# A hybrid decoder layer: transposing reads for the features of B and x, and SyncE's loads in program order

## The chip, the cores and the metric

The kernel runs on one core of a Trainium2 chip. The core has TensorE (PE; its weight loads are listed as PEld), VectorE (DVE), ScalarE (ACT), GpSimd (POOL) and SyncE (SP), which issues most DMAs. The metric is the device time of one launch in microseconds (us), lower is better.

## The reference

One decoder layer for 256 tokens of width 2048, in float32: a gated feed-forward network (FFN 1), a mixing block, a cross attention to 256 memory tokens and a second FFN, each added to the stream h, then a last RMSNorm. The mixing block has two halves that share one input projection `w_in`:

```python
proj = rmsnorm(h, mix_norm) @ w_in          # columns: u | v | z | x | B | C | dt
a = gelu(u) * (W_s @ rmsnorm(gelu(v)) + b)  # W_s causal in chunks of 128 tokens, 4 groups
x, B, C = split(silu(causal_conv4(x | B | C)))
dt = softplus(dt + dt_bias)
m = ssd_scan(x, dt, A, B, C) + d_skip * x   # 32 heads of 64, 8 groups, state 128, chunks of 128
m = rmsnorm(m * silu(z))
h = h + concat([a, m]) @ w_out
```

The scan works on two chunks of 128 tokens: inside a chunk a masked product of decays and scores with x * dt, between the chunks a state made of B and x * dt.

## The kernel before, in words

Every product in float32 is made of a high and a low half in float32r. A weight tile of 128 x 2048 elements is loaded (`load`, L136, on SyncE's queue, three buffers `raw`), cast to its high half by ScalarE (`high`, L166) and subtracted to its low half by VectorE (`low`, L179). Each projection is a loop over the inner dimension; one turn is a step, with its load, its split and its matmuls, and then `step()` (L82) runs what was put off with `later(fn, by)`: work that becomes due so many steps on. So the program order of all side work is written as due times. The scheduler of the language then orders each engine's instructions by their place in the program and by when it thinks they are ready; `behind(...)` holds an instruction behind named ones on its engine. Before the change, `behind` is used for the casts (`last_cast`) and for VectorE's splits (`last_split`, in `split_op`, L175), but not for DMAs.

The order of the mixing block:

- the B and C features, four column blocks of 512 with four steps each (`proj_feat`, L324): the output has features on partitions and tokens along the row. `gather` (L727) adds the banks, `conv_silu` (L739) makes the convolution and SiLU;
- `b_tokens` (L830): B's first chunk is wanted with tokens on partitions. Two steps after its column block, four TensorE transposes by an identity go into one PSUM bank and a copy brings them into `btok`, which `scan_states` reads much later;
- the x features, four column blocks of the same kind, into tiles `xf` of two feature tiles each. `x_tokens` (L847) turns them by four TensorE transposes each, two or three steps later, into one bank, and two copies bring them into `y[0]` and `y[1]`, the token tiles of the two chunks;
- v (16 steps, `proj_tok`, L212), then u (16 steps), then z (16 steps). The scan's four pieces are put off from the start of v: `scan_start` (L872) makes `xdt` = y * dt and y * d_skip for a chunk and reads the decay rows, `scan_decay` follows 1.5 steps later, `scan_apply` (L899) is due at 8, 12, 18.5 and 23;
- the output projection `w_out` (`add_sum`, L573), which reads the operands `at` (from a) and `mt` (from m).

There is a second way to turn a tile, used before for the FFNs' hidden tiles, for half of the mixing projection's operand and for a's operand: `turn_over` (L377) calls `write_planes` (L365), in which ScalarE copies the float32 tile into two planes of 16-bit halves (`halves`) and GpSimd writes them to DRAM (`planes`, four buffers); some steps later `read_turned` (L374) reads them with a transposing DMA on SyncE's queue into a tile `turned`, and again some steps later a `put` casts and splits that tile into an operand. The puts stand in line with the weights' casts and splits (`in_turn`, L388). The two due times are the pair `by`: (1, 4) for the hidden tiles, (2.5 + 1.5 n, 2.5) for chunk n of the mixing operand, (2.5 + 1.5 j, 2.5) for a's column j; the second of the two reads of a tile comes half a step after the first.

Of the kernel before, what the change touches and what calls it, by code (L numbers as in the profile page):

```python
# [8 lines left out]
F32 = mybir.dt.float32  # L9
F32R = mybir.dt.float32r  # L10
U16 = mybir.dt.uint16
# [6 lines left out]
P = 128  # L18
# [29 lines left out]
def hybrid_layer(ctx: ExitStack, tc: tile.TileContext, x, xt, mem, memt, w_gu1, w_dn1, w_in, w_s, w_out,  # L48
# [84 lines left out]
    PLAIN = {(0, 0): 0, (0, 1): 1, (1, 0): 2, (1, 1): 3}  # L133
    FOR_SUMS = {(0, 0): 0, (1, 0): 1, (1, 1): 2, (0, 1): 3}

    def load(w, r0, cs, at, fine=False):  # L136
        raw = wraw.tile([P, 2 * KP, NC], F32, name="raw")
        rows = w[r0:r0 + KP * P, :]
        if at is PLAIN and cs[1] == cs[0] + NC:
            nc.sync.dma_start(out=raw.rearrange("p (k j) n -> p k j n", j=2), in_=rows[:, cs[0]:cs[0] + 2 * NC].rearrange(  # L140
                "(k p) (j n) -> p k j n", p=P, j=2))
            return raw
        if fine:
            for (k, j), b in at.items():
                nc.sync.dma_start(out=raw[:, b, :], in_=rows[k * P:(k + 1) * P, cs[j]:cs[j] + NC])
            return raw
        for j, c in enumerate(cs):
            b, e = at[0, j], at[1, j]
            src = rows[:, c:c + NC]
            if e > b:  # L150
                nc.sync.dma_start(out=raw[:, b:e + 1:e - b, :], in_=src.rearrange("(k p) n -> p k n", p=P))
                continue
            for k, x in enumerate((b, e)):
                nc.sync.dma_start(out=raw[:, x, :], in_=src[k * P:(k + 1) * P, :])
        return raw

    def behind(instructions):

        order = ExitStack()
        for ins in instructions:  # L160
            order.enter_context(tc.issue_after(ins))
        return order

    last_cast = []

# [158 lines left out]
    def proj_feat(w, xts, n0):  # L324
        ps = {}
        n = D // P // (2 * KP)
        for i in range(n):
            raw = wraw.tile([P, 2 * KP, NC], F32, name="raw")
            nc.sync.dma_start(out=raw, in_=w[2 * i * KP * P:2 * (i + 1) * KP * P, n0:n0 + NC].rearrange(
                "(k p) n -> p k n", p=P))  # L330
            hi, lo = split(raw)
            order = [(k, c) for k in range(2 * KP) for c in range(4)]
            if i in (0, n - 1):
                order.sort(key=lambda kc: kc[1])
            for a in range(0, len(order), 4):
                for w_part in (hi, lo):
                    for k, c in order[a:a + 4]:
                        kt = 2 * i * KP + k
                        if c not in ps:
                            ps[c] = side("acc")  # L340
                        xt = xts[kt // KG][:, kt % KG, :]
                        w_kc = w_part[:, k, c * P:(c + 1) * P]
                        if w_part is hi:
                            matmul(ps[c], w_kc, xt, start=kt == 0)
                        else:
                            matmul(ps[c][:, S:], w_kc, xt[:, :S], stop=kt == D // P - 1)
            step()
        return [ps[c] for c in range(4)]
# [22 lines left out]
            nc.gpsimd.dma_start(out=planes[t * P:(t + 1) * P].rearrange("p b n -> p (b n)"), in_=halves)  # L371
        return planes

    def read_turned(to, planes, c0, n):  # L374
        nc.sync.dma_start(out=to, in_=planes[:, :, c0:c0 + n].rearrange("s b n -> (s b) n"), transpose=True)

    def turn_over(srcs, by, put):  # L377
        planes = write_planes(srcs)

        def fetch(q):  # L380
            to = half_k(F32, "turned")
            read_turned(to.bitcast(U16).rearrange("p (k s) -> p k s", k=KP), planes, q * P, KP * P)
            later(lambda: put(to.rearrange("p (k s) -> p k s", k=KP), q), by=by[1], bankless=True)

        for q in (0, 2):
            later(lambda q=q: fetch(q), by=by[0] + q / 4, bankless=True)

    def in_turn(src, last, op, c0=None):  # L388

# [66 lines left out]
    class Pieces(dict):  # L456
# [59 lines left out]
                                             op=ALU.subtract)  # L516
            return hi.ins, lo.ins

        def turn_later(self, srcs, by, c0=None, at=None):
            if at is None:  # L520
                at = self.due
                self.due += 2
            turn_over(srcs, by, lambda to, q: self.put(at + q // 2, to, q, c0))

        def later(self, srcs, c0=None, by=1):
            for q in (0, 2):
# [2 lines left out]
    class Normed:  # L529
# [8 lines left out]
        def chunk(self, n, by=1):  # L538
            srcs = [h[n][:, t, :] for t in range(NT)]
            if n < 2 and not isinstance(self.xts, Pieces):  # L540
                operand_turned(srcs, self.xts, f"xt_{self.name}{n}", self.c0 + n * KG, (2.5 + 1.5 * n, 2.5))
                self.stats(n)
            elif isinstance(self.xts, Pieces):

                for i in (2 * n, 2 * n + 1):
                    later(lambda i=i: self.xts.put(i, srcs, i % 2 * KP, self.c0 + n * KG),
                          self.bys.get(i, by))
                later(lambda: self.stats(n), self.stats_by)
            else:
                operand_later(srcs, self.xts, f"xt_{self.name}{n}", self.c0 + n * KG, by)  # L550
                self.stats(n)
# [59 lines left out]
    def ffn(nrm, w_gu, w_dn, done=None, each=None, fine=0, by_token=False):  # L611
        for c_from, c_to in ((0, 5), (5, 11)):
            kinds, turn = DN_KINDS[c_to - c_from]
            hts = Pieces(kinds, "hid", nrm.xts)
            for c in range(c_from, c_to):
                m = {}
                gs = []

                def mid(banks):
                    m["m1"], m["y"], m["z"], m["y2"] = parts_of(banks)  # L620

                def evac(t, j, ps):
                    g, u = (m["z"], m["y2"]) if t else (m["m1"], m["y"])
                    if j == 0:
                        total(g, ps, g, ALU.subtract if t else ALU.add)
                        nc.scalar.activation(g, g, AF.Silu, scale=nrm.rstd[:, t:t + 1])
                        return
                    total(u, ps, u)
                    nc.vector.scalar_tensor_tensor(out=g, in0=u, scalar=nrm.rstd[:, t:t + 1], in1=g,
                                                   op0=ALU.mult, op1=ALU.mult)  # L630
                    gs.append(g)

                if c == 0:
                    proj_sum(w_gu, 0, nrm.xts, FIRST_KINDS, (c * NC, DFF + c * NC), mid, evac, FIRST, fine)
                else:
                    proj_sum(w_gu, 0, nrm.xts, GU_KINDS, (c * NC, DFF + c * NC), mid, evac, GU_ORDER)
                hts.turn_later(gs, (1, 4))
            last = c_to == 11
            add_sum(w_dn, c_from * NC, hts, (kinds, kinds), turn, 0.5, done if last else None, each if last else None,
                    last and by_token)  # L640

# [186 lines left out]
    bt = slot([P, GROUPS, S], F32, "bt")  # L828
    ctr = slot([P, GROUPS, S], F32, "ct")
    def b_tokens(q):  # L830
        ps = side("tpose")
        for i in range(4):
            transpose(out=ps[:, i * P:(i + 1) * P], in_=bt[:, q * 4 + i, :P], identity=ident)
        nc.any.tensor_copy(out=btok[:, q * 4:q * 4 + 4, :], in_=ps.rearrange("p (g n) -> p g n", n=P))

    for c in range(4):
        xis = gather(proj_feat(w_in, nx.xts, B0 + c * NC))
# [3 lines left out]
        for i in range(4):  # L841
            conv_silu(xis[i], 16 + c * 4 + i, dst[:, (c % 2) * 4 + i, :])
        if c < 2:
            later(lambda c=c: b_tokens(c), by=2)
    y = [slot([P, HEADS, HD], F32, f"y{t}") for t in range(NT)]

    def x_tokens(c, i0, xf):  # L847
        tps = side("tpose").rearrange("p (t k s) -> p t k s", t=NT, k=2)
        for t in range(NT):
            for i in range(2):  # L850
                transpose(out=tps[:, t, i, :], in_=xf[:, i, t * P:(t + 1) * P], identity=ident)
        for t in range(NT):
            h0 = (c * 4 + i0) * 2
            nc.any.tensor_copy(out=y[t][:, h0:h0 + 4, :],
                               in_=tps[:, t].rearrange("p k (h d) -> p (k h) d", d=HD))

    for c in range(4):
        xis = gather(proj_feat(w_in, nx.xts, X0 + c * NC))
        for i0 in (0, 2):
            xf = half_k(F32, "xf").rearrange("p (k s) -> p k s", k=2)  # L860
            for i in range(2):
                conv_silu(xis[i0 + i], c * 4 + i0 + i, xf[:, i, :])
            later(lambda c=c, i0=i0, xf=xf: x_tokens(c, i0, xf), by=2 + i0 // 2)


    def per_head(ap, n):
# [5 lines left out]
    def scan_start(t, j):  # L872
        if j == 0:
            scan["xdt"] = scan[f"xdt{t}"] = xdt = slot([P, HEADS, HD], F32, "xdt")
            nc.vector.tensor_tensor(out=xdt, in0=y[t], in1=per_head(dt[:, t, :], HD), op=ALU.mult)
            nc.vector.tensor_tensor(out=y[t], in0=y[t], in1=per_head(rowb[:, 2, :], HD), op=ALU.mult)
        dec = slot([P, 16, P], F32, "dec")
        nc.gpsimd.dma_start(
# [60 lines left out]
                            base=0, channel_multiplier=-1)  # L939
    v = [slot([P, 4, NC], F32, f"v{t}") for t in range(NT)]  # L940
    ss_v = small.tile([P, NT, 4], F32, name="ss_v", bufs=1)
    for i, (by, to) in enumerate(((3, 8), (8, 12), (14, 18.5), (18.5, 23))):
        later(lambda i=i: scan_start(i // 2, i % 2), by=by)
        later(lambda i=i: scan_apply(i // 2, i % 2), by=to)
    for c in (0, 2):
# [31 lines left out]
    for c in (0, 2):  # L977
# [10 lines left out]

        proj_tok(w_in, 0, nx.xts, (U0 + c * NC, U0 + (c + 1) * NC), evac)
        for j in range(2):  # L990
            ats.turn_later(gss[j], (2.5 + 1.5 * j, 2.5))

    ss_m = small.tile([P, NT, 4], F32, name="ss_m", bufs=1)
    for c in (0, 2):
# [230 lines left out]
```

## Time and profile before

| | |
|---|---|
| time, median of 3 runs | 2428.43 us (2428.28 to 2432.98) |
| the profiled execution's own time | 2428.32 us |
| its span, first to last instruction | 2426.6 us |
| PE / DVE / ACT / POOL busy | 2413.6 / 2033.3 / 1361.4 / 65.4 us |
| granted TensorE clock | 0.999 |
| DMA traffic | 510 MB, mean 210 GB/s |
| transposing reads (`turned<-planes`) | 56 |

The page gives the busy time of each engine, the chain of work that ended last, and groups of instructions as "line engine operation out<-in". A timeline line has the start in us, the length in us, the engine, the line, the operation, out<-in, the tile's shape, a count, and in brackets the idle time of the engine before it with what ended it. For SPq the operation is the issue of a DMA, and the length is how long the queue was held by it and those merged with it. A line of the waits has who waited for whom, the sum in us, how many times and the longest. A line of the DMA issues has the count, the size of one and the median time from issue to landing. A matmul's printed length is longer than the distance to the next one's start, since they overlap. In the mixing block, the features lie from about 711 to 886 us, and v begins at 886.

### The profile page before, as it was taken

What the parts mean: (1) busy time and instruction counts of PE and PEld (TensorE: products, weight loads), DVE (VectorE), ACT (ScalarE), POOL (GpSimd) and SP (SyncE); (2) the same over time, 40 slices, a digit from 0 to 9 for tenths busy, and PEclk for the clock granted to TensorE, in tenths of its full rate; (3) what the DMA queues carried; (4) which work ended last, traced back from release to release, by engine and by line L of the source; (5) the groups of instructions that cost most, each with busy time, mean ns of one, the idle gap of its engine ahead of it and who ended that gap; (6) DMA issues with size and microseconds to landing.
All of it is one profiled execution on the core that took longest, in us unless ns stands there. A gap on an engine that the chain in (4) does not pass through costs nothing.

```text
span 2426.6 us, 29016 instructions
## 1 busy us (share of the span) xinstructions
PE 2413.6 (99%) x11141; PEld 2010.1 (83%) x11141; DVE 2033.3 (84%) x1943; ACT 1361.4 (56%) x1261; POOL 65.4 (3%) x124
## 2 busy tenths in 40 slices
PE   9999999999999999999999999999999999999998
PEld 7888888888888888788888888888888888888886
DVE  8999889999877777655698888778899988899997
ACT  7565446555656555445555655555556644556554
POOL 1000000000000000000000000000000000000000
PEclk9999999999999999999999999999999999999999
DMA  8777667677765555567557655555567776777774
GB/s 306 234 225 232 202 208 232 220 231 231 232 196 187 181 191 175 205 194 224 190 191 244 224 191 167 176 178 174 191 217 235 225 222 197 223 229 223 233 221 151
DMA packets 264844, 510.17 MB, mean 210 GB/s; under 512 B 75760, under 2 KB 77840, under 8 KB 263936
## 3 DMA queue, kind: packets, MB, share of 16 engines
q1 hardware_dynamic: 256224, 479.00, 62.6%
q0 software_dynamic: 7648, 28.26, 3.2%
q8 instruction: 87, 1.43, 0.2%
q10 hardware_dynamic: 832, 1.05, 0.1%
q14 instruction: 53, 0.43, 0.0%
HBM read 476.76 MB, written 16.81 MB: 203 GB/s over the span
## 4 chain that ended last, share of the span: by engine, by line
PE 95%; issue 3%; ACT 1%; DVE 1%; DMA 0%; SPq 0%; POOL 0%; POOLq 0%; DVEq 0%; ACTq 0%
PE acc L74 92%; PE tpose L77 1%; PE yp L74 1%; PE o L74 0%; PE logits L74 0%; PE mixed L74 0%; DVE lo L177 0%; DMA raw<-in_w_in 0%; ACT hi L169 0%; DMA raw<-in_w_gu 0%; PE dt L74 0%; PE scores L74 0%; PE yo L74 0%; PE st L74 0%; ACT hi L191 0%
## 5 line engine op out<-in xcount | busy, mean ns | idle before, releaser
L177 DVE TENSOR_TENSOR lo<-raw,hi 128x2048 fp32r<-128x2048 f32 (+2 forms) x449 | 945.2, 2107 | 242.5 <-PE acc L74 175.4
L169 ACT CAST hi<-raw 128x2048 fp32r<-128x2048 f32 (+1 forms) x437 | 785.0, 1798 | 488.6 <-PE acc L74 418.4
L74 PE MATMUL acc<-hi,xp_ffn 128*128 128x512 f32 x1824 | 574.3, 390 | 0.0
L74 PEld LDWEIGHTS acc<-hi,xp_ffn 128*128 128x128 f32 x1824 | 342.6, 188 | 71.1
L169 ACT CAST hi<-sum 128x2048 fp32r<-128x2048 f32 x117 | 224.1, 1915 | 294.8 <-DVE sum L177 153.4
L74 PE MATMUL acc<-lo,xp_ffn 128*128 128x512 f32 x912 | 355.0, 389 | 1.3 <-DVE h L661 1.3
L177 DVE TENSOR_TENSOR lo<-sum,hi 128x2048 fp32r<-128x2048 f32 x117 | 268.1, 2292 | 37.4 <-ACT hi L169 37.4
L74 PE MATMUL acc<-hi,hid 128*128 128x512 f32 x896 | 281.3, 389 | 0.0
L74 PE MATMUL acc<-hi,xt_mix 128*128 128x512 f32 x768 | 241.5, 393 | 0.0
L74 PEld LDWEIGHTS acc<-lo,xp_ffn 128*128 128x128 f32 x912 | 171.3, 188 | 37.5 <-DVE h L661 1.7
L600 DVE TENSOR_TENSOR part<-acc,part 128x512 f32<-128x512 f32 x272 | 180.5, 686 | 23.6 <-PE acc L74 8.5
L74 PEld LDWEIGHTS acc<-hi,hid 128*128 128x128 f32 x896 | 168.1, 188 | 34.9
L74 PE MATMUL acc<-lo,hid 128*128 128x512 f32 x448 | 174.3, 389 | 0.0
L74 PEld LDWEIGHTS acc<-hi,xt_mix 128*128 128x128 f32 x768 | 144.2, 188 | 30.8 <-issue 1.0
L177 DVE TENSOR_TENSOR sum<-sum,raw 128x512 f32<-128x512 f32 x234 | 161.6, 691 | 6.2
L74 PE MATMUL acc<-lo,xt_mix 128*128 128x512 f32 x384 | 149.7, 390 | 1.1 <-DVE lo L177 1.1
L74 PE MATMUL acc<-hi,xp_ffn1s 128*128 128x512 f32 x466 | 148.5, 389 | 0.0
L74 PE MATMUL acc<-hi,xp_ffn2s 128*128 128x512 f32 x466 | 148.5, 389 | 0.0
L177 DVE TENSOR_TENSOR sum<-raw 128x1024 f32<-128x1024 f32 x117 | 142.5, 1218 | 0.0
L74 PE MATMUL acc<-xt_mix,hi 128*128 128x512 f32 x512 | 140.5, 396 | 0.0
L74 PE MATMUL acc<-hi,hids 128*128 128x512 f32 x392 | 125.2, 389 | 0.0
L74 PE MATMUL acc<-hi,memt 128*128 128x512 f32 x384 | 123.4, 392 | 0.0
(297 smaller groups left out, 3164.6 us busy)
## 6 DMA issues: line engine op xcount, KB each, us to landing
raw<-in_w_gu SPq DMA_DIRECT2D x284, 512.0 KB, 4.6
raw<-in_w_in SPq DMA_DIRECT2D x80, 1024.0 KB, 5.1
raw<-in_w_dn SPq DMA_DIRECT2D x60, 1024.0 KB, 5.2
raw<-in_w_gu SPq DMA_DIRECT2D x136, 256.0 KB, 4.9
raw<-in_w_kv SPq DMA_DIRECT2D x24, 1024.0 KB, 5.2
raw<-in_w_out SPq DMA_DIRECT2D x21, 1024.0 KB, 5.2
planes<-halves POOLq DMA_DIRECT2D x56, 256.0 KB, 4.6
raw<-in_w_dn SPq DMA_DIRECT2D x28, 512.0 KB, 4.1
```

The lines of the kernel that those rows point to most:

```text
L74: return pe(nc.tensor.matmul(out, lhsT=lhsT, rhs=rhs, start=start, stop=stop))
L77: return pe(nc.tensor.transpose(out=out, in_=in_, identity=identity))
L169: last_cast[:] = [nc.scalar.copy(out=t[:, :n], in_=x[:, :n]).ins]
L177: last_split[:] = [nc.vector.tensor_tensor(**kw).ins]
L600: nc.vector.tensor_tensor(out=out, in0=a, in1=b, op=op)
```

## The change

It has four parts.

1. All weight loads and most transposing reads go through `from_dram`. From the first half of FFN 1 on (`line["kept"]`), each of them is held behind the one before it in the program, on SyncE's queue. The reads of the FFNs' hidden tiles and the new reads of B and x stay out of this line (`lined=False`).
2. The lined reads are one step apart (`q / 2`) and start later; their puts follow one step after: (6 + 2 n, 1) for the mixing operand, (6 + 2 j, 1) for a's.
3. `b_tokens` and `x_tokens` use no TensorE transposes and no PSUM any more: planes of 16-bit halves are written at once, and transposing reads bring them straight into `btok` (due one step later) and into `y[0]` (one step later) and `y[1]` (three steps later).
4. The scan's pieces are due later, and `xdt` stands in line with VectorE's splits.

```diff
+    line, last_load = {"kept": False}, []
+
+    def from_dram(lined=True, **kw):
+        with behind(last_load if lined and line["kept"] else ()):
+            ins = nc.sync.dma_start(**kw).ins
+        if lined:
+            last_load[:] = [ins]
...
-    def read_turned(to, planes, c0, n):
-        nc.sync.dma_start(out=to, in_=planes[:, :, c0:c0 + n].rearrange("s b n -> (s b) n"), transpose=True)
-
-    def turn_over(srcs, by, put):
+    def read_turned(to, planes, c0, n, lined=True):
+        from_dram(lined, out=to, in_=planes[:, :, c0:c0 + n].rearrange("s b n -> (s b) n"), transpose=True)
+
+    def turn_over(srcs, by, put, lined=True):
...
         for q in (0, 2):
-            later(lambda q=q: fetch(q), by=by[0] + q / 4, bankless=True)
+            later(lambda q=q: fetch(q), by=by[0] + (q / 2 if lined else q / 4), bankless=True)
...
-                operand_turned(srcs, self.xts, f"xt_{self.name}{n}", self.c0 + n * KG, (2.5 + 1.5 * n, 2.5))
+                operand_turned(srcs, self.xts, f"xt_{self.name}{n}", self.c0 + n * KG, (6 + 2 * n, 1))
...
-                hts.turn_later(gs, (1, 4))
+                hts.turn_later(gs, (1, 4), lined=False)
             last = c_to == 11
+            line["kept"] = True
...
     def b_tokens(q):
-        ps = side("tpose")
-        for i in range(4):
-            transpose(out=ps[:, i * P:(i + 1) * P], in_=bt[:, q * 4 + i, :P], identity=ident)
-        nc.any.tensor_copy(out=btok[:, q * 4:q * 4 + 4, :], in_=ps.rearrange("p (g n) -> p g n", n=P))
+        planes = dram.tile([P, 2, NC], U16, name="planes", tag="planes", bufs=4)
+        halves = tmp.tile([P, 2 * NC], U16, name="halves", tag="t2k")
+        halves_v = halves.rearrange("p (b g n) -> p b g n", b=2, g=4)
+        for g in range(4):
+            nc.scalar.copy(out=halves_v[:, :, g, :],
+                           in_=bt[:, q * 4 + g, :P].bitcast(U16).rearrange("p (n b) -> p b n", b=2))
+        nc.gpsimd.dma_start(out=planes.rearrange("p b n -> p (b n)"), in_=halves)
+        later(lambda: read_turned(btok[:, q * 4:q * 4 + 4, :].bitcast(U16), planes, 0, NC, False), by=1, bankless=True)
...
-            later(lambda c=c: b_tokens(c), by=2)
+            b_tokens(c)
...
     def x_tokens(c, i0, xf):
-        tps = side("tpose").rearrange("p (t k s) -> p t k s", t=NT, k=2)
-        for t in range(NT):
-            for i in range(2):
-                transpose(out=tps[:, t, i, :], in_=xf[:, i, t * P:(t + 1) * P], identity=ident)
-        for t in range(NT):
+        planes = write_planes([xf[:, i, :] for i in range(2)], S)
+
+        def fetch(t):
             h0 = (c * 4 + i0) * 2
-            nc.any.tensor_copy(out=y[t][:, h0:h0 + 4, :],
-                               in_=tps[:, t].rearrange("p k (h d) -> p (k h) d", d=HD))
+            read_turned(y[t][:, h0:h0 + 4, :].bitcast(U16).rearrange("p h d -> p (h d)"), planes, t * P, P, False)
+
+        for t in range(NT):
+            later(lambda t=t: fetch(t), by=1 + 2 * t, bankless=True)
...
-            later(lambda c=c, i0=i0, xf=xf: x_tokens(c, i0, xf), by=2 + i0 // 2)
+            x_tokens(c, i0, xf)
...
-            nc.vector.tensor_tensor(out=xdt, in0=y[t], in1=per_head(dt[:, t, :], HD), op=ALU.mult)
+            split_op(out=xdt, in0=y[t], in1=per_head(dt[:, t, :], HD), op=ALU.mult)
...
-    for i, (by, to) in enumerate(((3, 8), (8, 12), (14, 18.5), (18.5, 23))):
+    for i, (by, to) in enumerate(((4.5, 9), (9, 13), (15, 19.5), (19.5, 24))):
...
-            ats.turn_later(gss[j], (2.5 + 1.5 * j, 2.5))
+            ats.turn_later(gss[j], (6 + 2 * j, 1))
```

More of the change, by code (lines that the diff above doesn't have):

```diff
@@ L134, in hybrid_layer, with behind @@
     FOR_SUMS = {(0, 0): 0, (1, 0): 1, (1, 1): 2, (0, 1): 3}
+    def behind(instructions):
+        order = ExitStack()
+        for ins in instructions:
+            order.enter_context(tc.issue_after(ins))
+        return order
+    line, last_load = {"kept": False}, []
[4 more added lines that the diff above has]
+            last_load[:] = [ins]
     def load(w, r0, cs, at, fine=False):
@@ L139, in load @@
         if at is PLAIN and cs[1] == cs[0] + NC:
-            nc.sync.dma_start(out=raw.rearrange("p (k j) n -> p k j n", j=2), in_=rows[:, cs[0]:cs[0] + 2 * NC].rearrange(
+            from_dram(out=raw.rearrange("p (k j) n -> p k j n", j=2), in_=rows[:, cs[0]:cs[0] + 2 * NC].rearrange(
                 "(k p) (j n) -> p k j n", p=P, j=2))
@@ L144, in load @@
             for (k, j), b in at.items():
-                nc.sync.dma_start(out=raw[:, b, :], in_=rows[k * P:(k + 1) * P, cs[j]:cs[j] + NC])
+                from_dram(out=raw[:, b, :], in_=rows[k * P:(k + 1) * P, cs[j]:cs[j] + NC])
             return raw
@@ L150, in load @@
             if e > b:
-                nc.sync.dma_start(out=raw[:, b:e + 1:e - b, :], in_=src.rearrange("(k p) n -> p k n", p=P))
+                from_dram(out=raw[:, b:e + 1:e - b, :], in_=src.rearrange("(k p) n -> p k n", p=P))
                 continue
             for k, x in enumerate((b, e)):
-                nc.sync.dma_start(out=raw[:, x, :], in_=src[k * P:(k + 1) * P, :])
+                from_dram(out=raw[:, x, :], in_=src[k * P:(k + 1) * P, :])
         return raw
[L157 to L162, printed above, removed]
     last_cast = []
@@ L328, in proj_feat @@
             raw = wraw.tile([P, 2 * KP, NC], F32, name="raw")
-            nc.sync.dma_start(out=raw, in_=w[2 * i * KP * P:2 * (i + 1) * KP * P, n0:n0 + NC].rearrange(
+            from_dram(out=raw, in_=w[2 * i * KP * P:2 * (i + 1) * KP * P, n0:n0 + NC].rearrange(
                 "(k p) n -> p k n", p=P))
@@ L381, in fetch @@
             to = half_k(F32, "turned")
-            read_turned(to.bitcast(U16).rearrange("p (k s) -> p k s", k=KP), planes, q * P, KP * P)
+            read_turned(to.bitcast(U16).rearrange("p (k s) -> p k s", k=KP), planes, q * P, KP * P, lined)
             later(lambda: put(to.rearrange("p (k s) -> p k s", k=KP), q), by=by[1], bankless=True)
         for q in (0, 2):
-            later(lambda q=q: fetch(q), by=by[0] + q / 4, bankless=True)
+            later(lambda q=q: fetch(q), by=by[0] + (q / 2 if lined else q / 4), bankless=True)
     def in_turn(src, last, op, c0=None):
@@ L517, in sums, with turn_later @@
             return hi.ins, lo.ins
-        def turn_later(self, srcs, by, c0=None, at=None):
+        def turn_later(self, srcs, by, c0=None, at=None, lined=True):
             if at is None:
@@ L522, in turn_later @@
                 self.due += 2
-            turn_over(srcs, by, lambda to, q: self.put(at + q // 2, to, q, c0))
+            turn_over(srcs, by, lambda to, q: self.put(at + q // 2, to, q, c0), lined)
         def later(self, srcs, c0=None, by=1):
@@ L843, in hybrid_layer @@
         if c < 2:
-            later(lambda c=c: b_tokens(c), by=2)
+            b_tokens(c)
     y = [slot([P, HEADS, HD], F32, f"y{t}") for t in range(NT)]
     def x_tokens(c, i0, xf):
-        tps = side("tpose").rearrange("p (t k s) -> p t k s", t=NT, k=2)
+        planes = write_planes([xf[:, i, :] for i in range(2)], S)
+        def fetch(t):
+            h0 = (c * 4 + i0) * 2
+            read_turned(y[t][:, h0:h0 + 4, :].bitcast(U16).rearrange("p h d -> p (h d)"), planes, t * P, P, False)
         for t in range(NT):
-            for i in range(2):
-                transpose(out=tps[:, t, i, :], in_=xf[:, i, t * P:(t + 1) * P], identity=ident)
-        for t in range(NT):
-            h0 = (c * 4 + i0) * 2
-            nc.any.tensor_copy(out=y[t][:, h0:h0 + 4, :],
-                               in_=tps[:, t].rearrange("p k (h d) -> p (k h) d", d=HD))
+            later(lambda t=t: fetch(t), by=1 + 2 * t, bankless=True)
     for c in range(4):
```

## The prediction, made before the result was known

> **What bounds the kernel now.** I began with the page: its first part and the chain that ended last.
>
> ```profile
> span 2426.6 us, 29016 instructions
> ...
> PE 2413.6 (99%) x11141; PEld 2010.1 (83%) x11141; DVE 2033.3 (84%) x1943; ACT 1361.4 (56%) x1261; POOL 65.4 (3%) x124
> ...
> PE 95%; issue 3%; ACT 1%; DVE 1%; DMA 0%; SPq 0%; POOL 0%; POOLq 0%; DVEq 0%; ACTq 0%
> ```
>
> TensorE has work in 99% of the span and carries 95% of the chain. So an edit counts in two ways only: it takes matmul slots off TensorE, or it changes how long TensorE waits. Next, the view of the waits, for TensorE alone, shows how little waiting there is to win:
>
> ```profile
> PE idle L74 <- DVE idle L666: 1.3, 1, 1.3
> PE acc L74 <- DVE h L661: 1.3, 1, 1.3
> PE acc L74 <- DVE lo L177: 1.1, 1, 1.1
> ```
>
> Two of the three belong to L661 and L666, the opening of the kernel, which the change does not touch. The third, on a low half (L177), is the one that an edit could remove. Its place is in the timelines of TensorE, SyncE's queue and ScalarE around 1126 us, in the z projection:
>
> ```profile
> 1125.14 0.39 PE L74 MATMUL acc<-hi,xt_mix 128*128 128x512 f32 x1
> 1125.37 0.39 PE L74 MATMUL acc<-lo,xt_mix 128*128 128x512 f32 x1
> 1125.59 0.84 PE L74 MATMUL acc<-hi,xt_mix 128*128 128x512 f32 x3
> 1127.57 0.50 PE L74 MATMUL acc<-lo,xt_mix 128*128 128x512 f32 x1 [1.14 <-DVE lo L177]
> ...
> 1100.97 0.37 SPq L140 DMA_DIRECT2D raw<-in_w_in  x1
> 1102.59 11.62 SPq L375 DMA_TRANSPOSE turned<-planes  x4
> 1114.31 3.33 SPq L140 DMA_DIRECT2D raw<-in_w_in  x3
> ...
> 1120.59 1.91 ACT L169 CAST hi<-raw 128x2048 fp32r<-128x2048 f32 x1 [7.71 <-DMA raw<-in_w_in]
> ```
>
> Matmuls start 0.23 us apart here. Three begin at 1125.59, so the next is due at 1126.28 and comes at 1127.57: 1.3 us are lost. The cause is to be read upward: four transposing reads held SyncE's queue for 11.62 us, the next weight load went out only at 1114.31, ScalarE waited 7.71 us for it, and the low half came late. The same rows give the cover that this kernel has against a held queue: 11.62 us of hold cost 1.3 us, so some 10.3 us are hidden.
>
> **The transposes that leave TensorE.** In the view by tile, the identity transposes of x (`xf`) and of B (`bt`):
>
> ```profile
> L77 PE MATMUL tpose<-ident,xf x32: 270/272/276, 827.7 to 903.5; 128*128 128x128 f32 x32
> L77 PE MATMUL tpose<-ident,bt x8: 272/273/328, 734.7 to 759.9; 128*128 128x128 f32 x8
> ```
>
> Forty instructions in ten groups of four. Their duration is not what they cost, since matmuls overlap; the timeline of TensorE gives the price, by starts:
>
> ```profile
> 823.03 0.63 PE L74 MATMUL acc<-xt_mix,lo 128*128 128x256 f32 x4
> ...
> 824.43 0.64 PE L74 MATMUL acc<-xt_mix,lo 128*128 128x256 f32 x4
> ...
> 827.24 0.64 PE L74 MATMUL acc<-xt_mix,lo 128*128 128x256 f32 x4
> ...
> 827.72 0.60 PE L77 MATMUL tpose<-ident,xf 128*128 128x128 f32 x4
> ...
> 828.07 1.18 PE L74 MATMUL acc<-xt_mix,hi 128*128 128x512 f32 x4
> ...
> 829.09 0.63 PE L74 MATMUL acc<-xt_mix,lo 128*128 128x256 f32 x4
> ```
>
> Without transposes, one group of low matmuls follows the other after 1.40 us (823.03 to 824.43); with four transposes between, after 1.85 us (827.24 to 829.09). A group costs 0.45 us, ten cost 4.5 us. All of it is on the path, so **minus 4.5 us**.
>
> [...]
>
> **What stands in their place.** For each of the eight pairs of x tiles: two ScalarE copies into `halves`, two GpSimd writes, two reads on SyncE's queue; for each half of B: four ScalarE copies, one write and one read. That is 24 copies, 18 writes and 18 reads; the x reads have half of the bytes of today's. Sixteen evictions from PSUM and two of B go. The nearest rows:
>
> ```profile
> L369 ACT COPY halves<-gate x8: 1041/1048/1060, 1051.0 to 1102.0; 128x1024 uint16<-128x1024 uint16 x8
> ...
> 711.00:886.00 175.00, 175.00 (x1010) 152.08 (x1009) 128.67 (x201) 101.96 (x144) 1.63 (x3) 1.00 0.58 190
> ...
> planes<-halves POOLq DMA_DIRECT2D x56, 256.0 KB, 4.6
> ...
> turned<-planes SPq DMA_TRANSPOSE x56, 4.0
> ...
> L375 SPq DMA_TRANSPOSE turned<-planes x56: 1226/1290/4759, 61.3 to 2302.7; - x56
> ...
> SPq L375 <- DMA planes<-halves: 41.8, 28, 2.9
> ```
>
> A copy of half the columns takes between half of 1.05 us and all of it, so ScalarE gets 13 to 25 us. The window's row has the stretch and its length, then the busy time of PE, PEld, DVE, ACT and POOL: in the feature stage (711 to 886 us) ScalarE is busy for 102 of 175 us, so it hides them and only the reads wait for them. GpSimd is nearly idle there (1.63 us). SyncE's queue is what can hurt: a read holds it 1.3 us as a rule and 4.8 at worst, after up to 2.9 us of waiting for its planes, and the next weight load is queued behind. These reads stand outside the line, so one column block's four can come in a bunch, as the four at 1102 did. At 1.3 us each and one wait the bunch takes 8 us, under the cover of 10.3: I take **nothing**. The bounds are nothing and the worst hold, four times 4.8 = 19 us, less 10.3, for four blocks: 35 us. A gain is excluded, as TensorE shows no wait in this stage. I stay near the low end because the reads are half as large.
>
> The contention that goes with them is in the view of the DMA issues, over the whole run and then for 1095 to 1120 us alone:
>
> ```profile
> raw<-in_w_in SPq DMA_DIRECT2D x80, 1024.0 KB, 5.1
> ...
> raw<-in_w_in SPq DMA_DIRECT2D x5, 1024.0 KB, 7.8
> ```
>
> Beside four reads a load lands in 7.8 instead of 5.1 us. The 2.7 us are part of what the event at 1126 already paid, so they are in the cover and not counted again.
>
> [...]
>
> **The scan's start.** `xdt` reads all of y's first half and now stands by `split_op` between two low halves: begun after five instead of three steps of the v projection (due 4.5), it follows the low half of step 4 and precedes that of step 5. VectorE works in order: if y is late, the scaling of y (L876), the low half of step 5 and with it TensorE wait. The rows, from the timelines of ScalarE, VectorE, SyncE's queue and TensorE:
>
> ```profile
> 897.22 0.51 ACT L749 ACTIVATE xf<-cacc,col 128x256 f32<-128x256 f32 x1 [2.10 <-DVE cacc L747]
> ...
> 905.64 2.29 DVE L875 TENSOR_TENSOR xdt<-y,dt 128x2048 f32<-128x2048 f32 x1
> 907.96 2.29 DVE L876 TENSOR_TENSOR y<-y,rowb 128x2048 f32<-128x2048 f32 x1
> 910.17 2.29 DVE L177 TENSOR_TENSOR lo<-raw,hi 128x2048 fp32r<-128x2048 f32 x1
> ...
> 895.81 0.37 SPq L140 DMA_DIRECT2D raw<-in_w_in  x1
> ...
> 886.33 0.39 PE L74 MATMUL acc<-hi,xt_mix 128*128 128x512 f32 x1
> ...
> 914.53 1.05 PE L74 MATMUL scores<-ct,bt 128*128 128x128 f32 x8
> 915.34 0.48 PE L74 MATMUL acc<-hi,xt_mix 128*128 128x512 f32 x1
> ```
>
> The last x tile is ready at 897.7. Add a copy (0.6), the issue (0.3), a write (4.6) and a read (4.0): y is there at 907.2. Three operations of 2.3 us make the low half ready at 914.1. TensorE wants it one matmul into step 5. The five steps from 886.33 to 915.34 hold 0.8 us of scores and two transpose groups (0.9); without them step 5 begins at 913.6 and wants the low half at 913.8. So 0.3 us late on medians. The bounds are nothing (a scaling put behind the low half frees 2.3 us) and 7.8 us: write and read stretched as the loads above were (8.6 us by 7.8/5.1, 4.6 more) and the longest wait for planes, 2.9. Between them I take **plus 0.7 us**. The other scan steps move on by one step. The first decay gets two steps (10.9 us) instead of three before its use; it is three VectorE operations as large as `xdt` (6.9 us) and one exponential, which still fits. The last apply now meets the end of a u block, where gates and products want PSUM banks together; I take nothing for it, and a wait there would be new.
>
> **The line of loads.** An order costs no wait of its own, and load follows load today. The reads of the a operand now lie one step apart, with the put one step behind each, so one read of 1.3 us stands between two loads instead of four together. The event at 1126 goes: **minus 1.3 us**. The bounds are 1.3 and nothing. What is late next is the put itself, which ScalarE and VectorE take in order, with the casts of all later loads behind it. A load goes out 19.5 us before TensorE uses it (895.81, for the step at 915.34), so a read that stands just ahead of one lands, in 4 us, well before ScalarE comes to its put. The four reads for the mixing projection's operand move in the same way; TensorE does not wait there today, so nothing is to be won.
>
> **The sum.** The profiled execution took 2428.32 us, 1.7 more than its span and 0.1 below the median of the runs, 2428.43. 2428.3 - 4.5 - 1.3 + 0.7 = 2423.2, and 2423.3 against the median. About 0.2%, 4.9 us, is what a measurement of this kernel tells from no change; the forecast lies just beyond it.
>
> **The rivals.** *The reads' bunches cost what the bunch at 1102 cost.* 1.3 us in each of four x blocks, 5.2 us: 2428.5, no change. For it: the number of reads in a bunch is the same and they stand outside the line; against: half the bytes.
>
> *SyncE's queue becomes the bound of the x blocks.* One mechanism with a threshold: a bunch that holds the queue longer than 10.3 us. The reads at 1102 took 2.9 us each; with the longest wait before them, 2.9, a bunch holds 14.5 us and TensorE stands for 4.2, in four blocks 16.8 us: 2440, slower. It turns the sign from 2.7 us per block on, a hold of 13 us.
>
> *The line does not do its work.* The late low half stays or returns at the new place: 2424.6, no change.
>
> *A transpose costs its whole duration.* 40 times 0.272 is 10.9 us: 2416.9, faster. Against it stand the starts above; for it only the duration that the profile prints.
>
> **How the numbers follow.** Forecast 0.62, with its own range from 2421.8 (no late y, a little more won around the groups) to 2427; equal bunches 0.17; queue-bound 0.09; the line without effect 0.07; whole durations 0.05. Of the forecast's 0.62 some 0.45 lie beyond 4.9 us of gain: faster 0.50 with the whole durations, slower 0.09, the same 0.41. The range 2419.0 to 2431.0 leaves out the whole durations and the queue-bound case, 0.14 together, and a few hundredths of late y.
>
> **What would show it.** Right: no `xf` or `bt` transposes; the low groups of the x blocks 1.40 us apart throughout; no TensorE wait on L177 in the z projection; reads of the a operand single between loads; `xdt` begun near 907 less the 4 us won before. Wrong: TensorE waits on L177 between 820 and 900 with transposing reads of x in SyncE's queue before them (the bunches), or one at about 910 behind `xdt` (late y), or new waits in stages that have none today, which would mean that the order of loads matters.

## The result, and the profile after

The changed kernel took **2460.24 us** (median of 4 runs, 2457.69 to 2463.18) against 2428.80 for the kernel before beside it (2428.28 to 2432.98): 31.4 us slower, ratio 1.0126 with a 95% interval of 1.0108 to 1.0144. The forecast was 2423.3, the range ended at 2431.0. The profiled execution took 2460.04, its span is 31.7 us longer than the one before.

The page's first part, after:

```profile
span 2458.3 us, 29002 instructions
PE 2418.8 (98%) x11101; PEld 2011.4 (82%) x11101; DVE 2033.3 (83%) x1941; ACT 1368.5 (56%) x1269; POOL 78.9 (3%) x142
```

TensorE has 40 instructions fewer, and yet it is busy 5 us longer (2413.6 before). Its idle time grew too, as the view of the waits (TensorE alone) shows:

```profile
PE acc L74 <- ACT hi L177: 16.7, 2, 9.6
PE acc L74 <- DVE lo L185: 11.6, 4, 8.0
PE idle L74 <- DVE idle L675: 1.3, 1, 1.3
PE acc L74 <- DVE h L670: 1.1, 1, 1.1
```

The last two are the kernel's opening, as before. The first two are 28 us on halves of weights, five of the waits above 1 us, where there was one of 1.1. The timeline of TensorE says where they are and shows something else:

```profile
909.69 0.84 PE L74 MATMUL acc<-hi,xt_mix 128*128 128x512 f32 x3
918.57 0.79 PE L74 MATMUL acc<-lo,xt_mix 128*128 128x512 f32 x1 [8.03 <-DVE lo L185]
919.16 0.63 PE L74 MATMUL acc<-hi,xt_mix 128*128 128x512 f32 x1
919.58 0.63 PE L74 MATMUL acc<-lo,xt_mix 128*128 128x512 f32 x1
...
1099.46 0.61 PE L74 MATMUL acc<-hi,xt_mix 128*128 128x512 f32 x2
1107.16 0.79 PE L74 MATMUL acc<-hi,xt_mix 128*128 128x512 f32 x1 [7.09 <-ACT hi L177]
1109.49 0.79 PE L74 MATMUL acc<-lo,xt_mix 128*128 128x512 f32 x1 [1.53 <-DVE lo L185]
...
1155.89 0.61 PE L74 MATMUL acc<-hi,xt_mix 128*128 128x512 f32 x2
1166.14 0.79 PE L74 MATMUL acc<-hi,xt_mix 128*128 128x512 f32 x1 [9.63 <-ACT hi L177]
```

Three events, in v (918), u (1107) and z (1166). Behind each the matmuls start 0.43 us apart (919.16 to 919.58) where 0.23 is usual, for some five us. To price an event with all of that, I add up, for each matmul in a stretch, the distance to the next start less the usual distance for its shape, and call the sum the *lost time*. It is 10.9 us between 900 and 990, 12.9 between 1080 and 1130, 14.2 between 1130 and 1200, and within 0.25 of nothing in the rest of 600 to 1080. Before, the only loss in all of this was 1.4 at 1126, and that one is gone.

What left TensorE can be read as well. The low groups of an x block, after:

```profile
874.02 0.64 PE L74 MATMUL acc<-xt_mix,lo 128*128 128x256 f32 x4
875.43 0.63 PE L74 MATMUL acc<-xt_mix,lo 128*128 128x256 f32 x4
```

They are 1.40 apart throughout, so the ten groups of transposes gave back their 4.5 us. The account: 10.9 + 12.9 + 14.2 - 1.4 - 4.5 = 32.1 us, against 31.7 between the spans.

**The events at 1107 and 1166** begin in SyncE's queue. Its waits over the run, after; the first row's longest had been 2.9, the other two rows are new:

```profile
SPq L147 <- DMA planes<-halves: 90.5, 33, 16.5
SPq L147 <- DVE y L1013: 25.6, 2, 25.4
SPq L147 <- DVE at L417: 11.0, 1, 11.0
```

And its timeline:

```profile
1074.84 0.37 SPq L147 DMA_DIRECT2D raw<-in_w_in  x1
1086.32 1.23 SPq L147 DMA_TRANSPOSE turned<-planes  x1
1087.60 0.57 SPq L147 DMA_DIRECT2D raw<-in_w_in  x1
1104.72 1.29 SPq L147 DMA_TRANSPOSE turned<-planes  x1
1106.06 15.44 SPq L147 DMA_DIRECT2D raw<-in_w_in  x5
...
1131.27 0.37 SPq L147 DMA_DIRECT2D raw<-in_w_in  x1
1157.10 1.23 SPq L147 DMA_TRANSPOSE turned<-planes  x1
```

Three single reads stand for 11.0, 16.5 and 25.4 us before they start (at 1086, 1104 and 1157), and the weight loads behind them stand too: one load between 1074.84 and 1106.06, none between 1131.27 and 1157.10. TensorE eats one in 5.4 us (the load of 1074.84 from 1094.47 to 1099.9) and so has some 19 us of them ahead, and it runs dry. What ended the waits were a put of the operand (L417), a write of planes out of `halves`, and the product of y with its gate (L1013): each frees one of the six buffers that `turned`, `halves` and `gate` share. The last two come only at the end of a column block, and the weights of the next block stand behind the read.

At 1166 the load is what came last: it landed at 1164.16, and ScalarE began its cast at 1164.19. At 1107 ScalarE has a part in it as well:

```profile
1105.22 1.89 ACT L177 CAST hi<-raw 128x2048 fp32r<-128x2048 f32 x1
```

The load of 1087.60 had landed at 1095.28, but ScalarE has the block's gates and four copies into `halves` before its cast. The load after it landed only at 1114.05, so without that order TensorE would have stood one step later.

**The event at 918** has another chain. The timelines of VectorE and of SyncE's queue, after:

```profile
901.43 2.29 DVE L185 TENSOR_TENSOR lo<-raw,hi 128x2048 fp32r<-128x2048 f32 x1
914.02 2.29 DVE L185 TENSOR_TENSOR xdt<-y,dt 128x2048 f32<-128x2048 f32 x1 [10.30 <-DMA y<-planes]
916.23 2.28 DVE L185 TENSOR_TENSOR lo<-raw,hi 128x2048 fp32r<-128x2048 f32 x1
...
908.43 2.47 SPq L147 DMA_TRANSPOSE y<-planes  x2
```

`xdt` waits 10.3 us for the last read of y, issued at 908.43, and the low half that TensorE needs at 910.4 is queued behind it. This is the late y of the prediction: 914.0, where 907.2 was put on the clock of before, and v begins 3.4 us sooner here.

### The profile page after: what moved, and what is told of

It reads as the page before. It is cut to its first block, busy times and chain, and to the rows that moved or that the text cites. A ratio compares the mean times of both kernels' runs of the same rounds, so it can differ in the third digit from the quotient of the medians.

```text
span 2458.3 us, 29002 instructions
## 1 busy us (share of the span) xinstructions
PE 2418.8 (98%) x11101; PEld 2011.4 (82%) x11101; DVE 2033.3 (83%) x1941; ACT 1368.5 (56%) x1269; POOL 78.9 (3%) x142
## 5 line engine op out<-in xcount | busy, mean ns | idle before, releaser
L74 PE MATMUL acc<-hi,xt_mix 128*128 128x512 f32 x768 | 247.4, 401 | 16.7 <-ACT hi L177 16.7
```

The costliest lines, as they stand in the source:

```text
L74: return pe(nc.tensor.matmul(out, lhsT=lhsT, rhs=rhs, start=start, stop=stop))
```

## The experiments

**First, four single edits.** The theory: the line puts weight loads behind reads that lack a buffer (27.1 us), and y is late for the scan (10.9 us). The rivals: the reads' DMA work or their later due times are to blame, not the line. One run each, the kernel before beside them at 2429.07.

*No line.*

```diff
-            line["kept"] = True
+            line["kept"] = False
```

> The changed kernel with the line switched off: loads and lined reads may be ordered freely again; every due time is as changed. Theory (the line makes loads wait behind a read that waits for a buffer of the small pool): the two waits in u and z, 12.9 and 14.2 us of lost matmul time, go; the one at 910 stays, so about 2433 us. Rival (the reads themselves, by contention on the DMA engines, starve the loads): the same reads are made, so the time stays within 5 us of 2460.

Measured: 2449.61. Lost: 11.5 in v, 6.9 in u, 7.5 in z. Both expectations missed. The three long waits of SyncE are gone, yet half of the loss in u and z is still there. Four reads go out in one bunch again (from 1098.39, 12.56 us), now in the later steps, where SyncE waits for halves (6.3) and for the product with the gate (4.4). But the loads are not short this time: the weights that TensorE waits for had landed at 1092.2 and 1142.6, and ScalarE casts them at 1106.81 and 1157.75. Its timeline:

```profile
1104.39 0.62 ACT L416 CAST at<-turned 128x512 fp32r<-128x512 f32 x1
1104.92 1.99 ACT L377 COPY halves<-gate 128x1024 uint16<-128x1024 uint16 x2
1106.81 1.89 ACT L177 CAST hi<-raw 128x2048 fp32r<-128x2048 f32 x1
```

Puts and casts follow one another on ScalarE by the program (`in_turn`): the put at 1104.39 comes before this cast, and its read landed only at 1104.25. Before the change a cast ran between the block's copies (1095.47). Near 1157 a cast stands behind the put of a read that waited 3.6 us for the product with the gate and landed at 1155.6. So a late read costs without the line too, by way of its put; that is read from the rows, no run tested it alone. By size the line is half of the price, and the later due times make the other half.

*TensorE's transposes for B and x again* (the old `b_tokens` and `x_tokens`, the rest as changed).

> The changed kernel with B and x turned by TensorE transposes as before; line, due times and scan as changed. Theory (late y at 910 comes from the reads of x): that wait, 10.9 us lost, goes, the transposes' 4.5 us come back, the two waits in u and z stay: about 2454 us. Rival (the wait at 910 comes from where the scan and xdt were put): it stays, about 2465 us.

Measured: 2451.97. Lost in v: 0.05. SyncE's waits of 11.0, 16.5 and 25.4 us are the same to the tenth, and u and z lose 11.4 and 14.0. The event at 918 thus comes with the reads of x, the other two do not. The time is near the theory's 2454.

*Reads of B and x and the later scan alone: no line, the old due times of the operands' reads.*

```diff
-            line["kept"] = True
+            line["kept"] = False
...
-            later(lambda q=q: fetch(q), by=by[0] + (q / 2 if lined else q / 4), bankless=True)
+            later(lambda q=q: fetch(q), by=by[0] + q / 4, bankless=True)
...
-            ats.turn_later(gss[j], (6 + 2 * j, 1))
+            ats.turn_later(gss[j], (2.5 + 1.5 * j, 2.5))
```

> Only B and x by transposing reads and the later scan; no line, due times of the other reads as before. Theory: transposes minus 4.5, late y plus 10.9, the 1.4 us lost at 1126 stays: about 2435 us, with no TensorE wait in u and z but that one. Rival (x reads disturb the later stages too): waits of more than 5 us in u or z.

Measured: 2432.79. 8.9 lost in v, 1.4 in z as before the change, nothing in u.

*One buffer more (seven) for the shared pool* (and ten opening matmuls of half the width instead of five).

> The changed kernel with seven instead of six buffers in the small pool (the zero tile of the opening matmuls is made half as wide to have the room). Theory (lined reads wait for a buffer): both waits in u and z shrink by at least half, 2460 goes to 2447 or lower. Rival (the order of loads alone does it, whatever the buffers): the time stays within 4 us of 2460.

Measured: 2460.13, not a microsecond won. SyncE's waits, with seven buffers:

```profile
SPq L147 <- ACT gate L1011: 25.4, 2, 24.6
...
SPq L147 <- DVE gate L997: 18.7, 1, 18.7
```

The read that waited for the put now passes, and the next one waits for a gate. The wait had moved by one read; this run could not tell buffers from anything else that ends with a column block. It does show ScalarE's part at 1107: one load more gets through and lands at 1085.77, its cast still begins only at 1105.12, and 12.4 us are lost.

**Second, buffers that nobody else holds.** Four edits on one chip, the kernel before at 2428.64 (2427.44 to 2432.42).

*Own buffers for the lined reads of a's operand: the convolution's tile of rows, free by then.*

```diff
-    def turn_over(srcs, by, put, lined=True):
+    def turn_over(srcs, by, put, lined=True, own=None):
...
-            to = half_k(F32, "turned")
+            to = half_k(F32, "turned") if own is None else own[q // 2]
...
-            ats.turn_later(gss[j], (6 + 2 * j, 1))
+            ats.turn_later(gss[j], (6 + 2 * j, 1), own=own[2 * j:2 * j + 2])
```

> The changed kernel, but the lined reads of the operand of a get four buffers that nothing else holds at that time (the convolution's tile of rows, free after the features of x). Theory of the buffer (a read in line waits for one of the six buffers that the gates and halves hold, and the weight loads wait behind it): SyncE's waits of 11.0, 16.5 and 25.4 us go, and with them the 12.9 us lost by TensorE near 1099 and the 14.2 near 1156; the loss of 10.9 at 910 stays: 2460.0 - 27.1 = about 2433 (2430 to 2437). Theory of the order (a line alone, or the reads' longer transfers beside the loads, starve the weights): the losses near 1099 and 1156 stay, about 2460.

Measured: 2439.26 (2436.39 to 2441.90), ratio 1.0046 (1.0031 to 1.0061). SyncE's waits between 1060 and 1165 us, with own buffers:

```profile
SPq L147 <- DVE lo L185: 90.2, 18, 12.5
SPq L147 <- DMA planes<-halves: 1.0, 1, 1.0
```

The first row is a load that waits for the tile it fills to be used up, as loads should. The waits of 11.0, 16.5 and 25.4 are gone, u loses nothing, z 5.5 instead of 14.2 (in the profiled execution, the fastest of the four). That settles the buffer for the changed kernel: 21.6 of the 27.1 us, ScalarE's part at 1107 with it. The time is above the theory's 2430 to 2437. The 5.5 left are at 1150, where four products with gates (1140.7 to 1148.5) stand ahead of a low half on VectorE; that the puts, which now come there, push them together was not tested.

*The scan's four pieces later still.*

```diff
-    for i, (by, to) in enumerate(((4.5, 9), (9, 13), (15, 19.5), (19.5, 24))):
+    for i, (by, to) in enumerate(((7.5, 12), (12, 16), (16, 20.5), (20.5, 25))):
```

> The changed kernel, but the four pieces of the scan are due 3, 3, 1 and 1 later still (7.5 to 12, 12 to 16, 16 to 20.5, 20.5 to 25, in place of 4.5 to 9 and so on). Theory of the late y (the piece at 910 asks for a y whose last block is read only at 914): the loss of 10.9 us at 910 goes, the two near 1099 and 1156 stay: about 2449 (2447 to 2453). Rival (the reads of x hold back the loads of v's weights, and TensorE runs dry at that place whatever the scan does): the loss stays in the first part of v, about 2460.

Measured: 2459.38 (2459.26 to 2460.68), ratio 1.0126 (1.0112 to 1.0140): nothing won in time, but not by the rival. Around 910 nothing is lost, as the theory had it; a loss of 8.7 us has come up near 980 instead.

*Both.*

> Both at once: four own buffers for the lined reads of the operand of a, and the scan's pieces due 3, 3, 1 and 1 later. If the two theories hold and their places do not touch each other, all three losses go (10.9, 12.9 and 14.2 us) and what is left is the ten groups of transposes taken out of TensorE (-4.5) and the event at 1126 (-1.3): 2460.0 - 38.0 = about 2422 (2420 to 2426). If the loads are late for another reason, between 2433 and 2449.

Measured: 2437.05 (2436.83 to 2438.65), ratio 1.0034 (1.0022 to 1.0047): 8.8 lost near 980, 6.7 in z. That lies in the 2433 to 2449 given for late loads, but the loss near 980 is not one, as the next run shows.

*No line, old due times, the later scan.*

> The features of B and x by transposing reads, without the line and with the earlier due times of the reads of operands (2.5 and 4), and the scan's pieces due as late as in the run with a later scan. No read is in line, so nothing but the event at 1126 (1.3 us, as in the kernel before) should be left: 2428.4 - 4.5 = about 2424 (2422 to 2427). If taking the transposes out of TensorE is worth nothing: 2428. If the reads still hold up the loads in the first part of v: 2430 to 2435, as the run with the reads alone had it.

Measured: 2434.20 (2431.77 to 2435.23), ratio 1.0018 (1.0010 to 1.0027): 8.9 lost near 980, 1.5 in z. Its timelines of VectorE and TensorE:

```profile
977.77 0.69 DVE L920 TENSOR_TENSOR y<-yp,y 128x512 f32<-128x512 f32 x1 [7.43 <-PE yp L74]
979.55 0.69 DVE L920 TENSOR_TENSOR y<-yp,y 128x512 f32<-128x512 f32 x1 [1.09 <-PE yp L74]
980.16 2.28 DVE L925 TENSOR_TENSOR xdt<-xdt,dend 128x2048 f32<-128x2048 f32 x1
982.36 2.29 DVE L185 TENSOR_TENSOR xdt<-y,dt 128x2048 f32<-128x2048 f32 x1
...
984.63 2.28 DVE L185 TENSOR_TENSOR lo<-raw,hi 128x2048 fp32r<-128x2048 f32 x1
...
986.97 0.80 PE L74 MATMUL acc<-lo,xt_mix 128*128 128x512 f32 x1 [7.17 <-DVE lo L185]
```

The sum of the second piece and the start of the third are both due at 16, my own choice. VectorE waits 7.4 us for TensorE's `yp`, then does two sums, `xdt` times `dend` and the next `xdt`; the low half is behind them all. The time lies in the range given for reads that hold up the loads, for another reason.

**Third, the scan put where y is ready, and the line once more.** The kernel before beside them at 2429.18 (2427.62 to 2431.46).

*No line, old due times, the first piece as late as y is, the second piece's sum not with the third's start.*

```diff
-    for i, (by, to) in enumerate(((4.5, 9), (9, 13), (15, 19.5), (19.5, 24))):
+    for i, (by, to) in enumerate(((6.5, 10.5), (10.5, 14), (15, 19.5), (19.5, 24))):
```

> B and x by transposing reads, no line and the earlier due times, and the scan's pieces due 6.5 to 10.5, 10.5 to 14, 15 to 19.5 and 19.5 to 24: the first one only as late as y is (y's last block lands near 913, the multiplication behind the fourth low half comes at 912.6), the last two where the changed kernel has them, so that the second piece's sums are no longer due with the third piece's start. If the loss near 910 is the late y and the 8.9 us near 975 in the runs with the later scan is only this meeting of two pieces, both go: 2431.3 - 8.9 + 2 outside the span = about 2424 (2422 to 2427), 4 below the kernel before. If the later start itself costs the loss near 975 (a scan that ends too close to the end of v), about 2432.

Measured: **2425.51** (2423.99 to 2426.34, 11 runs), ratio 0.9983 (0.9975 to 0.9992), 3.7 us below the kernel before, with no overlap between the two sets of executions. All of TensorE's waits there but the two of the opening:

```profile
PE acc L74 <- DVE lo L185: 1.6, 1, 1.6
```

And VectorE's `xdt`, in its timeline:

```profile
913.18 2.29 DVE L185 TENSOR_TENSOR xdt<-y,dt 128x2048 f32<-128x2048 f32 x1 [0.85 <-DMA y<-planes]
```

`xdt` waits 0.85 us for y, and no one waits for `xdt`. This settles the loss near 910: it was y. The loss near 980 has shrunk from 8.9 to 1.8 us (near 974), but not because the two pieces were parted. VectorE still has them one behind the other, the low half last:

```profile
966.66 0.69 DVE L920 TENSOR_TENSOR y<-yp,y 128x512 f32<-128x512 f32 x1 [2.09 <-PE yp L74]
...
971.25 2.29 DVE L185 TENSOR_TENSOR xdt<-y,dt 128x2048 f32<-128x2048 f32 x1
973.45 2.29 DVE L185 TENSOR_TENSOR lo<-raw,hi 128x2048 fp32r<-128x2048 f32 x1
```

The kernel before has the same order there (960.05 to 966.90) and loses nothing. What differs is VectorE's wait for `yp`: none before, 2.1 us here, 7.4 in the run before this one, where TensorE comes to `yp` 11.8 us after the scores (964.05 to 975.84) instead of 6.4 (958.28 to 964.63). So of the expectation's two reasons the first held; for the second the edit moved all four pieces at once, and whether `yp` was late because its piece was due at the end of v, or for something else, stays open.

*The same scan and the line, own buffers, old due times.*

> The same scan, and the line kept, with four own buffers for the lined reads of the operand of a and the earlier due times. Theory: with buffers that nobody else holds and early reads a line costs nothing but takes the event at 1126 away (1.3 us): about 2423 (2420 to 2426). Rival: a line makes the loads wait for planes as well as for buffers, whatever the due times: a loss of 3 to 8 us stays at 1126 or 1156, 2427 to 2432.

Measured: 2441.49 (2437.39 to 2443.65), ratio 1.0046 (1.0032 to 1.0060), worse than the rival had it. Lost: 7.2 near 1070, 7.7 near 1120, 2.6 more than in the run just told before 870. SyncE's wait for planes over the run:

```profile
SPq L147 <- DMA planes<-halves: 117.9, 37, 21.2
```

And its timeline:

```profile
1086.61 5.81 SPq L147 DMA_DIRECT2D raw<-in_w_in  x2
1108.38 2.62 SPq L147 DMA_TRANSPOSE turned_hi<-planes  x2
1111.09 0.53 SPq L147 DMA_DIRECT2D raw<-in_w_in  x1
```

The buffers are free and a read still stands: in line, a read due early comes up while its planes are not written yet, since SyncE's loads run some 19 us ahead of the engines that write them (19.6 for the load of 1074.84 in the changed kernel). No load goes out between 1092.4 and 1111.1.

*The line, old due times, shared buffers, the changed kernel's scan.*

> The run with the reads and the scan only (2432.8), and the line kept: the line with the earlier due times and the shared buffers, and the changed kernel's scan. Theory of the buffer: early reads still need buffers that the halves and gates of the same column block hold, so waits of SyncE's queue of some 3 to 15 us appear and TensorE loses 5 to 15 us near 1100 and 1156: 2438 to 2448. Rival (only the late due times bring reads and held buffers together): nothing lost there, and the event at 1126 gone, about 2431.5.

Measured: 2445.31, one run. The time is inside what the theory gave, but not for its reason: the longest wait is again one for planes, 21.9 us, as with own buffers, and the losses are at 1075 (5.6) and 1125 (6.7), not at 1156. No read of a's operand waits for a gate or a put any longer.

The lost time in u and z (990 to 1200 us) side by side:

| reads of a's operand | due 2.5 and 4 | due 6 and 8 |
|---|---|---|
| no line, shared buffers | 1.5 | 14.5 |
| line, shared buffers | 12.7 | 27.2 |
| line, own buffers | 14.7 | 5.6 |

All of them have the changed kernel's scan but one: 14.7 is with the scan placed as in the fastest run, which itself loses 0.2. Own buffers with the late due times and no line were not run.

## Why the prediction was wrong

**"An order costs no wait of its own" is the step that failed.** It weighed the read's 1.3 us in the queue and the 4 us until it lands, and left out that an instruction in line waits for all that it needs: planes written and a buffer free. In line, every load behind pays. Due early, the read waits for planes (21.2); due late, for one of six buffers (up to 25.4), held until a column block ends, with the next block's weights behind the read. The same paragraph has a read land "well before ScalarE comes to its put". With the later due times and shared buffers it does not, and then the casts behind the put wait, with the line or without: 14.5 us are lost without it, 1.5 where the reads are due early. In place of -1.3 us the two changes of that paragraph cost 12.9 + 14.2 - 1.4 = 25.7, about half by each. With own buffers 21.6 of the 27.1 lost went. The prediction's signs of error had "new waits in stages that have none today, which would mean that the order of loads matters", but no rival had the mechanism, and "the line does not do its work" had the line as harmless.

**"Plus 0.7 us" for the late y: the mechanism was right, the size wrong.** It measured 10.9 us, past the bound of 7.8. The last tile of x was ready 19.1 us into v (902.06, v begun at 882.92) and not 11.4 (897.7 from 886.33). ScalarE's waits for loads between 880 and 925 us, after:

```profile
ACT hi L177 <- DMA raw<-in_w_in: 11.8, 4, 3.9
```

And those of SyncE's queue for planes, 870 to 925:

```profile
SPq L147 <- DMA planes<-halves: 23.6, 4, 8.3
```

SyncE waits up to 8.3 us for planes of x, loads go out late behind that, and ScalarE's casts wait for them, with the last tiles of the convolution queued behind. So the working took the last tile's time from before, though the reads themselves make it later. That this chain, and not another, made the tile late is read from the rows; no run tested it alone. Two more terms of it are the 2.9 us at half speed behind the wait, told below, and the write and read of y, 11.3 us together from the last copy's end (902.72) to the start of `xdt` (914.02) where 8.9 was taken with the issue. One term went the other way: the scaling of y came behind the low half (918.43), which the prediction had as a bound, and gave 2.3 us back.

**The transposes, -4.5 us: right.** The starts are 1.40 apart, and v, with eight of the ten groups before it, begins 3.4 us sooner (8 times 0.45 is 3.6). The run that keeps nothing else of the change but the reads and a scan that fits has a span of 2422.3, 4.3 below the 2426.6 of before; that is no second measure of the 4.5, since the event at 1126 is gone there and 1.8 us are lost near 974.

**The reads' bunches in the x blocks, nothing: right in its place.** Between 800 and 900 us no time is lost, in the changed kernel or in any of the runs. Their price came up later, as the late y.

**The event at 1126, -1.3 us: it went (1.4),** but a kernel without the line lost it as well when the scan fitted: 0.2 us are lost there in the fastest run. So the line was not needed for it; why that run no longer loses it was not tested.

## What to carry to other kernels

Before an instruction is put in program order on a queue that feeds the bound engine, list what it waits for (its source written, its target's buffer free, and who holds that buffer until when), not only how long it holds the queue: in line, each of these was a wait of the loads behind it here, up to 21.9 us for planes and 25.4 for a buffer. Where the buffer came free only at the end of a column block, the next block's loads started no sooner than that, and their lead of some 19 us was used up. And when a producer is moved to a longer path, its consumer's due time has to be set from the new path's end, with a look at whether the work that moves with it still finds its own inputs ready.

## What the hardware did that was not expected

A wait of TensorE cost more than its length here. The granted clock behind the 8.0 us wait, by stretches of the changed kernel (length, busy time of PE, PEld, DVE, ACT and POOL, then the clock):

```profile
918.00:920.00 2.00, 1.43 (x3) 1.16 (x4) 2.00 (x2) 0.00 (x0) 0.00 (x0) 0.50 0.29 29
920.00:923.00 3.00, 3.00 (x9) 2.30 (x8) 3.00 (x3) 0.00 (x0) 0.00 (x0) 0.50 0.87 325
...
924.00:926.00 2.00, 2.00 (x10) 1.63 (x9) 1.34 (x1) 0.00 (x0) 0.00 (x0) 0.99 0.87 250
```

For five us the clock is 0.50, and the event costs 10.9 us where the wait is 8.0. Behind a wait of 1.6 us, in the fastest run, it stays at 1.00 (975 to 979), and so it did behind the one of 1.1 in the kernel before (1127 to 1129); behind one of 3.8 us (the run with own buffers, at 1151) it is 0.50. So of these single waits the ones of 1.1 and 1.6 us cost no slow stretch, the ones of 3.8 and 8.0 did; where between 1.6 and 3.8 that changes was not shown. The length of the last wait is not the whole of it: in the run with the line, own buffers and the old due times, two waits of 2.1 and 1.8 us have one matmul between them (1068.85 to 1071.17). The matmul behind the first takes 0.49 us, as the one behind the 1.1 did in the kernel before (0.50); the one behind the second, shorter wait takes 0.79, as behind the 8.0, and the next ones start 0.43 us apart (1071.77 to 1072.19). The slow stretch behind the wait lasts 5.4 us in the changed kernel (918.57 to 924.0) and 3.1 in the run with own buffers (1151.12 to 1154.2); what sets its length was not tested.
